# A chain of five layers on one core: another layout of on-chip memory for the split weights and the normed inputs

## The chip, the cores and the metric

The kernel runs on one core of a Trainium2 chip. The metric is the device time of one execution in microseconds (us). TensorE (PE) multiplies matrices, VectorE (DVE) and ScalarE (ACT) work on tiles element by element, GpSimd (POOL) takes some smaller work, and SyncE (SP) issues the transfers (DMA) of the weights. Addresses in this text are KB from the start of a partition of the on-chip memory (SBUF); they are read from the two built programs.

## The reference

Five layers follow one another on 512 tokens of width 1024, in 32-bit arithmetic. This is the core of what is computed:

```python
x = first_block(...)                       # gated MLP branch and RWKV7 branch
for layer in range(2):
    a = rms_norm(h, norm_gains[layer, 0])
    m = mla_mixer(a, ...) if layer == 0 else hgrn2_mixer(a, ...)
    h = h + rms_norm(m, norm_gains[layer, 1])
    a = rms_norm(h, norm_gains[layer, 2])
    h = h + rms_norm(sq_relu_mlp(a, mlp_w1[layer], mlp_w2[layer]), norm_gains[layer, 3])

def sq_relu_mlp(h, w1, w2):                # w1: 1024 x 4096, w2: 4096 x 1024
    a = jax.nn.relu(h @ w1)
    return (a * a) @ w2
```

## The kernel before, in words

**Products.** Every large product is made of three: a 32-bit operand is split into a high part (rounded to the type fp32r) and the rest, and `mm3` (lines 181 to 184) issues high by high, high by low and low by high into one accumulator. A product of one block of 128 output columns, 512 tokens and a depth of 1024 is thus 8 chunks of 3 matmuls, 24 in all. A matmul has a moving operand, whose columns stream past, and a stationary one, which is loaded ahead. In the w1 products of the MLPs and in HGRN2's gates the activations move and the weights stand; in the MLP1's w2 product and in HGRN2's values it is the other way round.

**Weights.** `wchunk` (line 186) has a block of weights loaded by a transfer into a tile `raw` (4 KB of each partition, three buffers, pool `wr`). `wsplit` (line 173) then takes the next split slot: ScalarE casts `raw` to `wh` (line 140), VectorE subtracts to get `wl` (line 123). One slot is 8 KB, `wh` and `wl`. A slot can be written again once the last product that reads it is done. Three slots are there all the time; `wpool(2)` at the end of the MLA layer (line 1391) adds two, so that from MLA's output projection on there are five.

**Activations.** A layer's input is kept as eight chunks of 128 features by 512 tokens. There are two sets: `aH`, `aL` (pool `acts`, low addresses) and `bH`, `bL` (pool `acts2`, `new_acts(True)`, line 1085). The set `b` holds the normed input of both MLPs and of HGRN2; `a` holds the outputs of the mixers and the hidden activations of the MLPs.

**Order of work.** MLA's and HGRN2's output projections end in `mixer_out` (line 1394): `gemm_tail` makes four blocks of columns on all 512 tokens and four in two halves of 256 tokens (`gemm_halves`, line 201), so that `norms` (line 1098) can start on the first half: per half and chunk it scales the mixer's output (`mlom`), adds it to the residual (`res`), and splits the normed sum into `bH` (ScalarE) and `bL` (VectorE). Then `mlp` (line 1406) begins: `gemm_halves` on five blocks of columns of w1 (line 1488), whose accumulators are four `mm` tiles and one `sm` tile; it asks for five split weights before its first matmul in program order. 27 more w1 blocks follow as whole products of 512 tokens, between the w2 products. In MLP1, `second` (line 1442) asks for four split weights for each half of the output width. HGRN2's values take four per half as well.

The instructions of each engine are put in order by a scheduler that works from its own estimates of time; each engine then works through its list in that order.

**Memory.** Pools are stacked from both ends: constants, `acts`, `wr`, the split slots and the MLPs' own tiles from the low end, the residual, `acts2` and the mixers' tiles from the high end. With five slots and the MLPs' tiles both stacks together fill the memory.

Of the kernel before, what the change touches and what calls it, by code (L numbers as in the profile page):

```python
# [11 lines left out]
F32R = mybir.dt.float32r  # L12
# [8 lines left out]
P = 128  # L21
T = 512
# [13 lines left out]
SB = 1  # L36
MB = 1
BEGUN = 1
TT = ("sm", "sm", "mm", "mm")
NFILL = 61  # L40
ORDER = "r0 A0 k1 g0 k2 r1 g0 n0 r2 f11 g0 f1 t0 g1 m0 g1 k3 g1 g2 l0 g2 r3 g3 l1 g2 f7 l2 g3 l3 f2 l4 g3 l5 f5 l6 l7"
# [20 lines left out]
class Kern:  # L62
# [1020 lines left out]
            self.tt(acc[:, s], acc[:, s], sq, ALU.add, self.nc.gpsimd if k < 7 else None)  # L1083

    def new_acts(self, second=False):
        pool, t = (self.ap2, "b") if second else (self.ap_, "a")
        return [(self.tl(pool, [P, T], t + "H", F32R), self.tl(pool, [P, T], t + "L", F32R)) for _ in range(8)]

    def rstd(self, out, sums, n, fac=None):

# [42 lines left out]
    def gemm_tail(self, w, acts, K, evac, norm, begun=()):  # L1133
# [3 lines left out]
        for i in range(len(begun), 4):  # L1137
            self.gemm(w, i * P, acts, K, evac, i)
        self.gemm_halves(w, [i * P for i in range(4, 8)], acts, K, evac, range(4, 8), norm, TT)

# [11 lines left out]
    def mla(self):  # L1152
# [234 lines left out]
            self.psums([("mm", 2), ("sm", 4)], 1)  # L1387
        wx.close()
        self.mlx.close()
        self.wpool(2)  # L1390
        self.ap2 = self.ctx.enter_context(self.pool("acts2", 8))
        self.mixer_out("mlo", w_o, Acts(oa), 1, 2, begun)

    def mixer_out(self, nm, w_o, o, gpost, gpre, begun=()):
# [131 lines left out]
    def hgrn(self):  # L1526
# [3 lines left out]
        with ExitStack() as ox:  # L1530
            oa = self.new_acts()
            with ExitStack() as mx:
# [199 lines left out]
                w_o = I["hgrn_w_o_2"][0]  # L1732
                begun = [self.products(w_o, i * P, Acts(oa), 8, "mm") for i in range(BEGUN)]
                self.psums([("mm", 2), ("sm", 4)], 1)
        self.mixer_out("hgm", w_o, Acts(oa), 5, 6, begun)

    def build(self):
        tc, ctx = self.tc, self.ctx
        self.consts()
        self.sp = ctx.enter_context(self.pool("small", 2, side="left"))  # L1740
        self.ap_ = ctx.enter_context(self.pool("acts", 8, side="left"))
        self.WU, self.leng, self.wprio = 8 * P, self.nc.vector, 400
        self.wr = ctx.enter_context(self.pool("wr", 3, side="left"))
        self.wx = []
        self.wslots, self.wn = [], 0
        self.wpool(3)
        self.block1()
        self.mla()
        self.mlp(0)
        self.hgrn()  # L1750
        self.mlp(1)
# [33 lines left out]
```

## Time and profile before

| | us |
|---|---|
| median of three runs (lowest, highest) | 1616.99 (1616.04, 1617.93) |
| the profiled execution, its own time | 1615.6 |
| its span, first to last instruction | 1613.8 |
| TensorE busy | 1542.8 |
| VectorE busy | 939.0 |
| ScalarE busy | 713.3 |
| GpSimd busy | 329.5 |

In the trace MLA's output projection ends at 605 us, MLP0 at 965, HGRN2 at 1244, and MLP1 goes to the end. A matmul's record in the trace is longer than the time that it takes from the next one, since matmuls overlap; what a matmul costs in a stream without gaps is the distance from its start to the start of the next. In the rows, a name without its number stands for all tiles of a kind: `mm<-bH,wh` is a matmul into an `mm` accumulator with a `bH` tile moving and a `wh` tile standing. Each row ends, in brackets, with the idle time before it and what ended it, if there was any.

### The profile page before, as it was taken

Reading aid. Unit: us, or ns where it says so; the run is one execution under the profiler, and the core shown is the slowest. Engines: PE = TensorE matmul, PEld = TensorE weight load, DVE = VectorE, ACT = ScalarE, POOL = GpSimd, SP = SyncE. Lnnn points to the kernel's source line nnn. Section 1 sums busy time; section 2 is a strip of 40 time slices with the busy share of each in tenths; the row PEclk is TensorE's granted clock in tenths of the full one; section 3 lists DMA queues with packets and bytes.
Section 4 is the critical chain, followed back from the end, with each engine's and each line's share of the span. In section 5 each row is a group of like instructions: output and inputs, shape, how many; then the busy total and the mean of one; then the engine's idle time right before and its main releaser. Section 6 shows DMA issues by size and latency. Waiting matters only on the chain. (4 is left out here: it accounts for less than half of the span.)

```text
span 1613.8 us, 21901 instructions
## 1 busy us (share of the span) xinstructions
PE 1542.8 (96%) x8293; PEld 1305.5 (81%) x8293; DVE 939.0 (58%) x1644; ACT 713.3 (44%) x1297; POOL 329.5 (20%) x459
## 2 busy tenths in 40 slices
PE   5987979999999999999999999999999999999998
PEld 4766768889978899888888887888888988888886
DVE  7797595678667739334343447667754824333445
ACT  3533314655565646333232335667745624322232
POOL 4464732224310023000000033223323200000000
PEclk9998989999999999999999999999999999999999
DMA  9732445544123132333333322322213223231421
GB/s 289 215 97 86 78 130 144 178 132 119 51 70 94 29 105 80 104 103 93 91 93 104 92 91 67 104 79 66 66 53 110 87 79 118 74 110 66 123 86 53
DMA packets 272893, 161.69 MB, mean 100 GB/s; under 512 B 29465, under 2 KB 253316, under 8 KB 272788
## 3 DMA queue, kind: packets, MB, share of 16 engines
q1 hardware_dynamic: 271492, 157.33, 34.2%
q0 software_dynamic: 1152, 2.70, 0.5%
q8 instruction: 65, 1.06, 0.3%
q14 instruction: 40, 0.33, 0.1%
q10 hardware_dynamic: 144, 0.26, 0.0%
HBM read 147.42 MB, written 11.53 MB: 98 GB/s over the span
## 5 line engine op out<-in xcount | busy, mean ns | idle before, releaser
L140 ACT CAST wh<-raw 128x1024 fp32r<-128x1024 f32 (+3 forms) x244 | 242.8, 996 | 466.0 <-PE mm L143 371.2
L123 DVE TENSOR_TENSOR wl<-raw,wh 128x1024 fp32r<-128x1024 f32 (+2 forms) x228 | 272.6, 1197 | 288.1 <-ACT wh L140 284.0
L143 PE MATMUL mm<-bL,wh 128*128 128x512 f32 (+1 forms) x752 | 282.2, 378 | 1.0 <-DVE bL L133 1.0
L143 PE MATMUL mm<-bH,wl 128*128 128x512 f32 (+1 forms) x752 | 281.7, 377 | 0.0
L143 PE MATMUL mm<-bH,wh 128*128 128x512 f32 (+1 forms) x752 | 279.4, 379 | 0.1
L143 PE MATMUL mm<-aH,wh 128*128 128x512 f32 (+1 forms) x656 | 241.0, 369 | 12.3 <-DVE gt L133 9.5
L143 PE MATMUL mm<-aH,wl 128*128 128x512 f32 (+1 forms) x656 | 236.8, 362 | 1.4 <-DVE wl L123 1.4
L143 PE MATMUL mm<-aL,wh 128*128 128x512 f32 (+1 forms) x656 | 237.7, 364 | 0.0
L143 PEld LDWEIGHTS mm<-bL,wh 128*128 128x128 f32 x752 | 141.1, 188 | 29.4 <-DVE bL L133 1.8
L143 PEld LDWEIGHTS mm<-bH,wl 128*128 128x128 f32 x752 | 141.1, 188 | 27.7
L143 PEld LDWEIGHTS mm<-bH,wh 128*128 128x128 f32 x752 | 139.2, 188 | 28.0 <-ACT hg_vt L137 0.5
L143 PEld LDWEIGHTS mm<-aH,wh 128*128 128x128 f32 x656 | 125.2, 191 | 34.4 <-DVE gt L133 10.5
L143 PEld LDWEIGHTS mm<-aH,wl 128*128 128x128 f32 x656 | 125.2, 191 | 20.7 <-DVE wl L123 1.9
L143 PEld LDWEIGHTS mm<-aL,wh 128*128 128x128 f32 x656 | 125.7, 192 | 18.3 <-issue 0.7
L143 PE MATMUL mm<-wh,aH 128*128 128x512 f32 x288 | 113.5, 396 | 1.5 <-ACT aH L140 1.5
L143 PE MATMUL mm<-wh,aL 128*128 128x512 f32 x288 | 112.8, 393 | 0.0
L143 PE MATMUL mm<-wl,aH 128*128 128x512 f32 x288 | 112.6, 393 | 0.0
L140 ACT CAST aH<-t 128x512 fp32r<-128x512 f32 (+1 forms) x74 | 41.1, 564 | 75.7 <-DVE t L123 75.5
L123 POOL TENSOR_TENSOR mlpt<-mlpt,sq 128x256 f32<-128x256 f32 (+1 forms) x9 | 11.9, 1320 | 306.6 <-ACT sq L137 306.6
L245 POOL TENSOR_TENSOR mlpss<-mlpss,pwm 128x1 f32<-128x1 f32 x4 | 2.2, 547 | 322.0 <-DVE mlpss L128 322.0
L123 DVE TENSOR_TENSOR aL<-t,aH 128x512 fp32r<-128x512 f32 (+1 forms) x74 | 45.1, 617 | 36.2 <-ACT aH L140 36.2
L143 PEld LDWEIGHTS mm<-wh,aH 128*128 128x128 f32 x288 | 54.6, 190 | 12.7 <-ACT aH L140 1.9
(545 smaller groups left out, 2819.7 us busy)
## 6 DMA issues: line engine op xcount, KB each, us to landing
raw<-in_mlp_w_dram SPq DMA_DIRECT2D x128, 512.0 KB
raw<-in_hgrn_w_in_dram SPq DMA_DIRECT2D x32, 512.0 KB
raw<-in_w_in_dram SPq DMA_DIRECT2D x23, 512.0 KB
ada<-in_w_ada_dram SPq DMA_DIRECT2D x16, 512.0 KB
raw<-in_w_out_dram SPq DMA_DIRECT2D x10, 512.0 KB
raw<-in_w_ada_dram SPq DMA_DIRECT2D x8, 512.0 KB
raw<-in_mla_w_o_dram SPq DMA_DIRECT2D x8, 512.0 KB
raw<-in_hgrn_w_o_dram SPq DMA_DIRECT2D x8, 512.0 KB
```

The lines of the kernel that those rows point to most:

```text
L123: self.st((eng or self.nc.vector).tensor_tensor(out=out, in0=a, in1=b, op=op))
L140: self.st(self.nc.scalar.copy(out=out, in_=in_))
L143: i = self.nc.tensor.matmul(out, l, r, start=start, stop=stop, **kw)
L245: self.nc.gpsimd.tensor_tensor(out=out, in0=a, in1=cst[: a.shape[0], :n], op=ALU.pow)
```

## The change

Three pools are laid out in another way. The raw weights (`wr`) go to the high end. From MLA's output projection on there is one split slot more than the three, not two, so four in all. `acts2` is divided: five chunks of `bH` and `bL` go to a new pool `acts2l` at the low end, three and the tiles `bs` stay at the high end. No instruction is added or removed on any engine.

```diff
--- before.py
+++ after.py
@@ -36,6 +36,7 @@
 SB = 1
 MB = 1
 BEGUN = 1
+LOW = 5
 TT = ("sm", "sm", "mm", "mm")
 NFILL = 61
 ORDER = "r0 A0 k1 g0 k2 r1 g0 n0 r2 f11 g0 f1 t0 g1 m0 g1 k3 g1 g2 l0 g2 r3 g3 l1 g2 f7 l2 g3 l3 f2 l4 g3 l5 f5 l6 l7"
@@ -1083,8 +1084,8 @@
             self.tt(acc[:, s], acc[:, s], sq, ALU.add, self.nc.gpsimd if k < 7 else None)
 
     def new_acts(self, second=False):
-        pool, t = (self.ap2, "b") if second else (self.ap_, "a")
-        return [(self.tl(pool, [P, T], t + "H", F32R), self.tl(pool, [P, T], t + "L", F32R)) for _ in range(8)]
+        pools, t = ([self.ap2l] * LOW + [self.ap2] * (8 - LOW), "b") if second else ([self.ap_] * 8, "a")
+        return [(self.tl(z, [P, T], t + "H", F32R), self.tl(z, [P, T], t + "L", F32R)) for z in pools]
 
     def rstd(self, out, sums, n, fac=None):
 
@@ -1387,8 +1388,11 @@
             self.psums([("mm", 2), ("sm", 4)], 1)
         wx.close()
         self.mlx.close()
-        self.wpool(2)
-        self.ap2 = self.ctx.enter_context(self.pool("acts2", 8))
+        self.wpool(1)
+        self.ap2 = self.ctx.enter_context(self.pool("acts2", 8 - LOW))
+        self.wx.append(ExitStack())
+        self.wslots.append([])
+        self.ap2l = self.wx[-1].enter_context(self.pool("acts2l", LOW, side="left"))
         self.mixer_out("mlo", w_o, Acts(oa), 1, 2, begun)
 
     def mixer_out(self, nm, w_o, o, gpost, gpre, begun=()):
@@ -1740,7 +1744,7 @@
         self.sp = ctx.enter_context(self.pool("small", 2, side="left"))
         self.ap_ = ctx.enter_context(self.pool("acts", 8, side="left"))
         self.WU, self.leng, self.wprio = 8 * P, self.nc.vector, 400
-        self.wr = ctx.enter_context(self.pool("wr", 3, side="left"))
+        self.wr = ctx.enter_context(self.pool("wr", 3))
         self.wx = []
         self.wslots, self.wn = [], 0
         self.wpool(3)
```

Where the tiles lie in the MLPs and in HGRN2, in KB:

| | before | after |
|---|---|---|
| `aH`, `aL` | 17.75 to 49.75 | the same |
| `raw` | 49.75 to 61.75 | 211.97 to 223.97 |
| split slots | 61.75 to 101.75 (five) | 49.75 to 81.75 (four) |
| `bH`, `bL`, chunks 0 to 4 | 171.97 to 203.97 (with 5 to 7) | 81.75 to 101.75 |
| `bH`, `bL`, chunks 5 to 7 | | at the high end, from 179.97 |

The shift of the residual and the mixers' tiles by 12 KB moves some tiles of block 1 and MLA across the middle of the memory too: most of MLA's eight input tiles `zH`, from 102.84 up before, come to lie below 102.

The order of the instructions changes in two places at the entry of each MLP. **TensorE at the entry of the first MLP**, before: the first row of the fifth block of w1 columns (accumulator `sm_1142`; the four others are `mm_1138` to `mm_1141`, and `wh_1136`, `wl_1137` are its split weights), and the end of the entry.

```order
L143 MATMUL mm_1141_6313<-bH_1038_5745,wh_1133_6300 128x256
L143 MATMUL sm_1097_6193<-ident_66,mlow_5766 128x128 x2
L143 MATMUL sm_1142_6314<-bH_1030_5737,wh_1136_6306 128x256
L143 MATMUL mm_1138_6310<-bL_1039_5746,wh_1124_6282 128x256
L143 MATMUL mm_1138_6310<-bH_1038_5745,wl_1125_6283 128x256
L143 MATMUL mm_1139_6311<-bL_1039_5746,wh_1127_6288 128x256
...
L143 MATMUL mm_1141_6313<-bL_1045_5752,wh_1133_6300 128x256
L143 MATMUL mm_1141_6313<-bH_1044_5751,wl_1134_6301 128x256
L143 MATMUL sm_1142_6314<-bH_1030_5737,wh_1136_6306 128x256
...
L143 MATMUL mm_1166_6622<-bH_1030_5737,wh_1164_6618 128x512
```

In the changed kernel, the end of the entry:

```order
L144 MATMUL mm_1140_6315<-bH_1044_5754,wl_1131_6298 128x256
L144 MATMUL mm_1141_6316<-bL_1045_5755,wh_1133_6303 128x256
L144 MATMUL mm_1141_6316<-bH_1044_5754,wl_1134_6304 128x256
L144 MATMUL sm_1142_6317<-bH_1030_5740,wh_1136_6309 128x256
L144 MATMUL sm_1142_6317<-bL_1031_5741,wh_1136_6309 128x256
L144 MATMUL sm_1142_6317<-bH_1030_5740,wl_1137_6310 128x256
...
L144 MATMUL sm_1142_6317<-bH_1044_5754,wl_1137_6310 128x256
L144 MATMUL sm_1142_6317<-bH_1030_5740,wh_1136_6309 128x256
...
L144 MATMUL mm_1166_6625<-bH_1030_5740,wh_1164_6621 128x512
```

Before, the fifth block's 24 matmuls on the first 256 tokens are strewn among those of the four others, and 24 on the second half stand at the end. Now all 48 stand at the end, behind the last matmul of the other four.

**ScalarE at the same place**, before: the cast of the fifth block's weights, `wh_1136`, and that of the next block, `wh_1164`, with the norm's last activations (`bH_1044`, `sqh_1105`) ahead of it.

```order
L137 ACTIVATE bH_1032_5739<-res1_563_3122,pc_632 128x256
L137 ACTIVATE sqh_1085_6030<-res1_563_3122 128x256
L140 CAST wh_1136_6306<-raw_1135_6304 128x1024
L140 COPY mlom7_5764<-mm_1077_5901 128x256
...
L137 ACTIVATE sqh_1105_6245<-res7_569_3128 128x256
L140 CAST aH_1155_6463<-t_1157_6465 128x256
L140 CAST wh_1164_6618<-raw_1163_6616 128x1024
L137 ACTIVATE t_1158_6495<-mm_1138_6310 128x256
L140 CAST wh_1172_6664<-raw_1171_6662 128x1024
```

In the changed kernel:

```order
L138 ACTIVATE bH_1044_5754<-res7_569_3128,pc_632 128x256
L138 ACTIVATE sqh_1105_6248<-res7_569_3128 128x256
L141 CAST wh_1136_6309<-raw_1135_6307 128x1024
L141 CAST wh_1164_6621<-raw_1163_6619 128x1024
L141 CAST wh_1172_6667<-raw_1171_6665 128x1024
L141 CAST wh_1179_6705<-raw_1178_6703 128x1024
L138 ACTIVATE t_1157_6468<-sm_1142_6317 128x256
```

The cast of `wh_1136` has moved from the middle of the norm to behind its last activation: with four slots it takes the one of the first block (`mm_1138`), while before it took a slot that MLA's output projection had freed. VectorE's subtraction `wl_1137` moves with it. The entry of the second MLP changes in the same way.

## Rows read from the trace of the kernel before

**Rows 1.** The page: busy time by engine, 40 slices, chain by line.

```profile
PE 1542.8 (96%) x8293; PEld 1305.5 (81%) x8293; DVE 939.0 (58%) x1644; ACT 713.3 (44%) x1297; POOL 329.5 (20%) x459
...
PE   5987979999999999999999999999999999999998
...
PEclk9998989999999999999999999999999999999999
...
PE mm L143 19%; DVE mlpy L123 0%; PE sm L143 0%; DVE mlpy L133 0%; PE sm L149 0%; ACT t L137 0%; POOL mlpss L245 0%; DVE mlpss L123 0%; DVEq L1781 0%; POOLq L1781 0%; DVE mlpss L133 0%; DVE mlpss L128 0%; ACTq L137 0%
```

**Rows 2.** Stretches, TensorE: us, busy us (count), granted clock, DMA share, GB/s.

```profile
665.97:698.61 32.64, 32.64 (x145) 1.00 0.40 111
704.21:737.81 33.60, 33.60 (x145) 1.00 0.33 95
1304.46:1309.90 5.44, 5.44 (x25) 1.00 0.00 0
1005.12:1015.63 10.51, 10.51 (x47) 1.00 0.25 68
```

**Rows 3.** Groups by form, TensorE: count, busy us, mean ns, idle before.

```profile
L143 PE MATMUL mm<-bH,wh 128*128 128x512 f32 x624 | 248.7, 399 | 0.1
...
L143 PE MATMUL mm<-wh,bH 128*128 128x512 f32 x64 | 25.2, 399 | 1.4 <-ACT bH L137 1.4
```

**Rows 4.** Timeline of TensorE: start us, duration us; bounds of two half products.

```profile
587.20 0.28 PE L143 MATMUL mm<-aH,wh 128*128 128x256 f32 x1
...
590.08 0.28 PE L143 MATMUL mm<-aH,wh 128*128 128x256 f32 x1
...
634.57 0.28 PE L143 MATMUL sm<-bH,wh 128*128 128x256 f32 x1
...
637.41 0.40 PE L143 MATMUL mm<-bH,wh 128*128 128x512 f32 x1
```

**Rows 5.** Stretch, MLP0 entry: us; PE, PEld, DVE, ACT, POOL busy; clock; DMA.

```profile
605.30:632.40 27.10, 25.48 (x208) 24.65 (x208) 26.47 (x58) 16.44 (x42) 12.81 (x14) 1.00 0.14 40
```

**Rows 6.** Timeline of VectorE, MLP0 entry.

```profile
608.07 1.76 DVE L123 TENSOR_TENSOR wl<-raw,wh 128x1024 fp32r<-128x1024 f32 x1
...
627.78 0.41 DVE L123 TENSOR_TENSOR t<-t 128x256 f32<-128x256 f32 x1
...
631.23 0.42 DVE L123 TENSOR_TENSOR bs<-bs,sqh 128x256 f32<-128x256 f32 x1 [0.63 <-POOL bs L123]
631.57 0.87 DVE L133 SCALAR_TENSOR_TENSOR bL<-res,pc,bH 128x256 fp32r<-128x256 f32 x2
...
634.09 1.23 DVE L123 TENSOR_TENSOR wl<-raw,wh 128x1024 fp32r<-128x1024 f32 x1 [1.25 <-ACT wh L140]
```

**Rows 7.** Timelines of ScalarE and TensorE, MLP0 entry.

```profile
633.00 1.05 ACT L140 CAST wh<-raw 128x1024 fp32r<-128x1024 f32 x1 [1.96 <-PE mm L143]
...
632.11 0.38 PE L143 MATMUL mm<-bL,wh 128*128 128x256 f32 x1 [0.17 <-DVE bL L133]
...
632.80 0.39 PE L143 MATMUL mm<-bH,wl 128*128 128x256 f32 x2
```

**Rows 8.** Timelines of VectorE and TensorE, MLP1 entry.

```profile
1270.04 0.88 DVE L133 SCALAR_TENSOR_TENSOR bL<-res,pc,bH 128x256 fp32r<-128x256 f32 x2
...
1275.88 0.40 PE L143 MATMUL mm<-bH,wh 128*128 128x512 f32 x1
```

**Rows 9.** Timelines of ScalarE and VectorE, first half change of w2 in MLP1.

```profile
1312.87 1.05 ACT L140 CAST wh<-raw 128x1024 fp32r<-128x1024 f32 x1 [0.35 <-PE mm L143]
...
1317.93 1.05 ACT L140 CAST wh<-raw 128x1024 fp32r<-128x1024 f32 x1 [1.80 <-DMA raw<-in_mlp_w_dram]
...
1313.96 2.59 DVE L123 TENSOR_TENSOR wl<-raw,wh 128x1024 fp32r<-128x1024 f32 x2 [0.18 <-ACT wh L140]
```

**Rows 10.** Waits of TensorE, 525 to 565 us: total us, times, longest us.

```profile
PE sm L143 <- ACT P L137: 1.1, 1, 1.1
```


## The prediction, made before the changed kernel was run

> **What bounds the kernel now.** I first read the page. TensorE is busy for 1542.8 us of the span of 1613.8, in the slices from the fifteenth on at nine tenths or more, and its clock stands at the upper of its two levels, 2.4 GHz, in nearly all slices; the parts of the chain that ended last which the page names by line are TensorE's matmuls of line 143 almost alone [rows 1]. So from MLA's output projection on, time is the number of matmuls times the distance between their starts, plus TensorE's few gaps. The change leaves the number of instructions as it is. It can act in three ways: on that distance, on the gaps where a split weight comes too late, and on what TensorE finds to do in a gap.
>
> Then I measured the distance in stretches without a gap. Six w2 products of MLP0, with `aH` and `aL` moving, take 32.64 us for 144 matmuls, 226.7 ns each; six w1 products, with `bH` and `bL` moving, 33.60 us, 233.3 ns [rows 2]. (A count in those rows holds one or two matmuls more, which had begun before.) The clock is 1.00 in both, the weights are of the same five slots, and the form is the same. What differs is where the moving tile lies: `a` up to 49.75 KB, `b` from 171.97 up. Two more stretches set the rule: in MLP1's w2 product the slots move, up to 101.75 KB, and `a` stands: 5.44 us for 24, 226.7 ns. In HGRN2's values the slots move too, but `b` stands: 10.51 us for 45, 233.5 ns [rows 2]. So a 512-column matmul costs 6.6 ns more when either operand lies high, and addresses up to 101.75 count as low. The five moved chunks end exactly there, on addresses that slots held before, and the trace has those at the low price.
>
> The Trainium skill speaks against this: "TensorE: Matmul & The Clock Gate", section "Wait — 56ns, not 53.3ns?", gives the distance from the number of columns and the clock alone, 215.7 ns at 512 columns, with no term for the address. By that rule the layout would bring nothing at the matmuls, and only the lost slot would be left. The trace does not agree with it: 226.7 and 233.3 ns stand side by side at one clock [rows 2].
>
> **The sum, part by part.**
>
> *Five chunks at the low end, whole products.* 624 matmuls of `bH` by `wh` with 512 columns, and as many of each of the two other forms, are 1872, or 78 products of 24: 27 in each MLP, 24 for HGRN2's gates [rows 3]. A product costs 5.60 us high and 5.44 low; five eighths of its matmuls change, 0.10 us. 78 times 0.10 is **7.8 us** less. HGRN2's values are 64 times three, 192 matmuls [rows 3]; 120 of them change, 120 times 6.6 ns is **0.8 us** less. All of it lies on TensorE's path. Bounds: nothing, if one high chunk among eight spoils the product, to 8.6; I take the upper end, because the price follows each matmul's operands in all four stretches.
>
> *The same for the halves.* A half product of 256 columns takes 2.88 us from `a` (587.20 to 590.08) and 2.84 from `b` (634.57 to 637.41) [rows 4], so here low is dearer, by 1.7 ns a matmul. The MLPs' first five blocks are 2 times 5 times 48, 480 matmuls, of which 300 change: **0.5 us** more, between nothing and 0.5.
>
> *One slot less, at the entry of the MLPs.* This is the price. VectorE, working through the norm, is busy for 26.47 of 27.10 us there, TensorE for 25.48 [rows 5]: the norm sets the pace, and TensorE used its spare time for the fifth block's first half. Before, the last `bL` lands at 632.44 (631.57 and 0.87) [rows 6] and the entry ends 4.97 us later, at 637.41 [rows 4]. In the changed kernel the fifth block has no slot until `mm_1138` is done. VectorE's list holds as many `wl` ahead of the last `bL` as before (that of 608.07 is then the fourth block's) and one `t` less, 0.34 us [rows 6], so the last `bL` but one lands at about 631.7. Behind it, in TensorE's order, stand 14 matmuls up to `mm_1138`'s last, at 0.118 us [rows 4]: 633.4. The cast began 0.2 us after that matmul's start (632.80 to 633.00) [rows 7], so now at 633.6; 1.05 later it is done, VectorE takes 1.23 more [rows 6, 7], and at about 635.95 the fifth block's third matmul, the first by `wl`, can go. 46 matmuls at 0.118 are 5.4 us: the entry ends at 641.4, **4.0 us** later. The entry of MLP1 has the same shape, 1270.92 to 1275.88, 4.96 us [rows 8], so both cost **8.0 us**. Bounds for one entry: 2.5, when only the 2.84 us of the half that lost its cover less the `t` come out, to 4.6, if VectorE, which now has `t` earlier in its list, waits once more for 0.6 us as it does at 631.23 [rows 6]. I take 4.0, since each step of it has a row.
>
> *One slot less, elsewhere.* At w2's half changes in MLP1 four split weights are wanted at once, and four slots are left. The last of the four is cast at 1317.93, when its transfer lands, not when a slot comes free, so it stays; the first three shift by one release, 1.36 us, and the first `wl` then ends at about 1315.2 (1313.96 and 1.23) [rows 9], just ahead of the first matmul by it, at 1315.8 (1309.90 and 5.44 of a product, two matmuls on) [rows 2]. Nothing, then; at most one such step late at each of seven changes, some 0.5 us each, 3.5. At HGRN2's entry the four values' weights shift by one release as well; nothing, or one `wl` of 1.23 us on the norm's path. In whole products a cast and a subtraction, 2.3 us [rows 6, 7], fit well within the three products of 5.5 us that other slots hold.
>
> *MLA's tail.* The output projection's second block gets a fresh slot, so some of its matmuls move forward into the attention's tail, where TensorE waits for 1.1 us once [rows 10]. I take **0.4 us** less, between 1.1 less and 0.5 more, if the cast comes ahead of a softmax step.
>
> *Raw weights at the high end.* VectorE and ScalarE read them there; no row has that at another address. Nothing; at most the 0.5 just named.
>
> Sum: 7.8 and 0.8 and 0.4 less, 0.5 and 8.0 more, **0.5 us less**: 1615.1 for the profiled execution of 1615.6. The median of the runs stands 1.4 above that execution, at 1616.99, so I forecast **1616.5**: no change. (Some 0.2%, 3.2 us, is what a measurement of this kernel can tell from none.)
>
> **The rivals.**
>
> *The entries cost less, and it is faster.* If the fifth block's slot comes free earlier than I read, or the shorter list lets the norm end earlier, each entry costs 2.5: the sum is 3.5 less, and with the whole 1.1 at MLA's tail 4.2: **1612.8**. For it: VectorE's spare time at the entry is only 0.6 us, so each instruction that leaves its list counts. Against: the chain of cast, `wl` and 46 matmuls has no slack in it.
>
> *The low price does not come, and it is slower.* If one high chunk in eight keeps the whole product at 5.60 us, or the price hangs on something else than the address, the 8.6 us go and 8.1 stay: **1625**. It decides at the first whole w1 product: 5.60 us or 5.50. Against: rows of either role of the operand agree. The skill's rule above would end here too.
>
> *Slots are short elsewhere.* HGRN2's entry and w2's half changes cost 1.2 and 3.5: 4.7 on top of the sum: **1621**. For it: the margin at a half change is 0.6 us. Against: the scheduler has put other blocks' matmuls between.
>
> **How the numbers follow.** My forecast gets 0.43; the cheaper entries 0.32, the missing low price 0.13, the shortage elsewhere 0.12. So faster 0.32, within 0.2% 0.43, slower 0.25. The forecast's own bounds (entries 2.5 to 4.6 each, tail 1.1 less to 0.5 more) give 1613 to 1619. With the neighbouring cases the range goes from 1611.5 to 1622.5; it leaves out the missing low price and extremes, under 2 in 10.
>
> **What would show it.** Whole w1 products at 5.50 us (a matmul 226.7 ns on five chunks, 233.3 on three) confirm the gain; 5.60 refutes it, 5.44 would mean that the edge lies elsewhere. At MLP0's entry the stretch from the last `bL` to the first 512-column matmul should grow from 4.97 to about 9.3 us, with TensorE waiting for `wl` once. A gap of over 0.3 us at 1315 or at each half change after it speaks for the third rival. If the gain is there and the entry is not longer, my reading of the slots is wrong.

## The result, and the profile after

The changed kernel takes 1634.68 us (median of four runs, 1632.57 to 1635.60), the kernel before 1617.46 in the same comparison: a ratio of 1.0102, 95% interval 1.0084 to 1.0120. It is slower by some 17 us; I had forecast 1616.5, within 1611.5 and 1622.5. The span of the profiled execution grew from 1613.8 to 1632.7.

From the page of the kernel after, the lines that answer to [rows 1]:

```profile
PE 1545.9 (95%) x8293; PEld 1310.7 (80%) x8293; DVE 940.7 (58%) x1644; ACT 712.5 (44%) x1297; POOL 329.2 (20%) x459
...
PE   5987889999999998999999999999999899999998
...
PEclk9998989999999999999999999999999999999999
...
PE mm L144 61%; PE sm L144 6%; PE po L144 2%; DVE wl L124 2%; DVE bL L134 1%; PE sc L144 1%; PE mg L144 1%; DVE TV L124 1%; PE sd L144 1%; DVE acc L134 1%; DVE res L124 1%; DVE acc L124 1%; PE ss L144 1%; DVE bz L124 1%; ACT wh L141 1%
```

TensorE is busy 3 us longer, though no matmul was added, and over 15 us more of the span it stands still. Of the chain that ended last, three quarters are now matmuls and 14% VectorE's work. In the slices the loss is faint: the sixteenth and the thirty-second, which hold the two entries of the MLPs, fall from 9 to 8.

The start of each product in both traces tells where the offset between them arises (how much later the changed kernel starts the same product). It is 0.6 us at the end of block 1 and 1.6 when the first w1 matmul of MLP0 starts (605.35 and 606.92). At the end of that entry it is 11.2, and falls to 8.9 through MLP0 and to 7.4 through HGRN2's gates. HGRN2's output projection takes it to 9.4, MLP1's entry to 20.9, and MLP1's products bring it down to 18.9. So both entries lose, 9.6 and 11.5 us where I had 4.0 each, HGRN2's output projection loses 2.0, and the products win some 6.

Stretches of TensorE, as [rows 2]: six w1 products, then the last part of MLP0's entry and of MLP1's.

```profile
715.34:748.38 33.04, 33.04 (x145) 1.00 0.34 97
645.70:648.60 2.90, 2.90 (x16) 0.50 0.67 182
1291.50:1296.80 5.30, 5.30 (x25) 0.50 0.32 106
```

The products cost 33.04 us for six where they cost 33.60, 5.51 each: the gain is there, at nearly the size forecast (5.50). The two other stretches are what nobody asked for: the granted clock stands at 0.50, the lower of the two levels, and 256-column matmuls go by at some 213 ns instead of 118.

The entry of MLP0 in the timelines of VectorE, TensorE and ScalarE, as [rows 6, 7]:

```profile
633.99 0.87 DVE L134 SCALAR_TENSOR_TENSOR bL<-res,pc,bH 128x256 fp32r<-128x256 f32 x2
...
637.44 3.50 DVE L124 TENSOR_TENSOR wl<-raw,wh 128x1024 fp32r<-128x1024 f32 x3 [2.52 <-ACT wh L141]
644.05 1.23 DVE L124 TENSOR_TENSOR wl<-raw,wh 128x1024 fp32r<-128x1024 f32 x1 [3.12 <-ACT wh L141]
```

```profile
606.92 0.28 PE L144 MATMUL mm<-bH,wh 128*128 128x256 f32 x1
...
634.52 0.39 PE L144 MATMUL mm<-bL,wh 128*128 128x256 f32 x1 [0.35 <-DVE bL L134]
...
637.46 0.39 PE L144 MATMUL sm<-bH,wh 128*128 128x256 f32 x1 [0.31 <-ACT wh L141]
...
638.72 0.39 PE L144 MATMUL sm<-bH,wl 128*128 128x256 f32 x1 [0.76 <-DVE wl L124]
...
644.36 0.39 PE L144 MATMUL sm<-bH,wh 128*128 128x256 f32 x1 [2.75 <-ACT t L138]
...
648.57 0.63 PE L144 MATMUL mm<-bH,wh 128*128 128x512 f32 x1
```

```profile
633.05 0.40 ACT L138 ACTIVATE sqh<-res 128x256 f32<-128x256 f32 x1
636.36 2.95 ACT L141 CAST wh<-raw 128x1024 fp32r<-128x1024 f32 x3 [2.90 <-PE mm L144]
642.98 1.04 ACT L141 CAST wh<-raw 128x1024 fp32r<-128x1024 f32 x1 [3.67 <-DMA raw<-in_mlp_w_dram]
643.93 0.38 ACT L138 ACTIVATE t<-sm 128x256 f32<-128x256 f32 x1
```

SyncE, which issues the transfers, at the same place:

```profile
638.69 6.98 SPq L162 DMA_DIRECT2D raw<-in_mlp_w_dram  x4
```

The last `bL` lands at 634.86 (633.99 and 0.87). TensorE finishes the four blocks' part of the entry, waits for the cast of the fifth block's weights (0.31) and for its `wl` (0.76), and works through the first half of the fifth block. Up to here it is the chain that I had added up: with the second half behind it at 0.118 us a matmul the entry would end at 644.3, 9.4 us after the last `bL`; I had 9.3. But TensorE then waits 2.75 us for an activation `t`, and ends at 648.57. That `t` is the eviction of the fifth block's first half. In ScalarE's list it stands behind four casts, and the fourth cast waits 3.67 us for a transfer, to 642.98. That transfer was issued at 638.69, when VectorE's first subtraction (637.44 and some 1.2) had just ended.

MLP1's entry, VectorE and TensorE, as [rows 8]:

```profile
1280.28 0.87 DVE L134 SCALAR_TENSOR_TENSOR bL<-res,pc,bH 128x256 fp32r<-128x256 f32 x2
...
1291.50 0.58 PE L144 MATMUL sm<-bH,wh 128*128 128x256 f32 x1 [3.60 <-ACT t L138]
...
1296.79 0.63 PE L144 MATMUL mm<-bH,wh 128*128 128x512 f32 x1
```

15.6 us from the last `bL` (1281.15) to the end, where it was 4.96; the wait for `t` is 3.6 us, and the whole second half goes at the lower clock.

### The profile page after: what moved, and what is told of

Same layout as the page of the kernel before. It is cut to its first block, busy times and chain, and to the rows that moved or that the text cites. A ratio compares the mean times of both kernels' runs of the same rounds, so it can differ in the third digit from the quotient of the medians.

```text
span 1632.7 us, 21900 instructions
## 1 busy us (share of the span) xinstructions
PE 1545.9 (95%) x8293; PEld 1310.7 (80%) x8293; DVE 940.7 (58%) x1644; ACT 712.5 (44%) x1297; POOL 329.2 (20%) x459
## 4 chain that ended last, share of the span: by engine, by line
PE 76%; DVE 14%; issue 3%; DMA 3%; ACT 2%; POOL 1%; SPq 1%; DVEq 0%; POOLq 0%; ACTq 0%
PE mm L144 61%; PE sm L144 6%; PE po L144 2%; DVE wl L124 2%; DVE bL L134 1%; PE sc L144 1%; PE mg L144 1%; DVE TV L124 1%; PE sd L144 1%; DVE acc L134 1%; DVE res L124 1%; DVE acc L124 1%; PE ss L144 1%; DVE bz L124 1%; ACT wh L141 1%
```

## The experiments

My theory after the result had two parts: the lost slot costs some 25 us, and the low chunks give some 7 of them back. And, inside the first part: three raw buffers hold weights that wait for slots, so that the fourth transfer is issued too late, and ScalarE's list passes its delay on. The first five kernels test this, the others the price of a matmul.

**Raw weights at the high end, nothing else**

```diff
-        self.wr = ctx.enter_context(self.pool("wr", 3, side="left"))
+        self.wr = ctx.enter_context(self.pool("wr", 3))
```

> One part alone: only the raw weights go to the high end; five slots, all chunks of the normed input high. Theory (the lost slot costs some 25 us, the low chunks give some 7 back): within 2 us of the kernel before, w1 products at 5.60 us. Rival (raw weights at the high end delay the casts, the subtractions or the transfers): slower by 5 us or more, with longer casts (over 1.05 us) or longer subtractions (over 1.23 us).

Measured: 1618.50 us against 1617.24, ratio 1.0004 (0.9992 to 1.0015), w1 products at 5.60 us. Casts and subtractions of 1024 columns are as long as before (means of 1047 and 1254 ns, before 1049 and 1254). Moving the raw weights costs nothing that can be measured.

**Four slots, nothing else**

```diff
-        self.wpool(2)
+        self.wpool(1)
         self.ap2 = self.ctx.enter_context(self.pool("acts2", 8))
```

> One part alone: four split slots instead of five from the output projection of MLA on, all else as in the kernel before. Theory: about 24 to 26 us slower than before (1641 to 1643), since the entries of the two MLPs cost 9.6 and 11.5 us and both output projections some 2, and nothing comes back. Rival (the loss comes from where the tiles lie, or from the raw weights): slower by less than 12 us.

Measured: 1641.44 us, ratio 1.0141 (1.0125 to 1.0158), 24.2 more than before. The ScalarE timeline at MLP0's entry has the same picture as the changed kernel's, with everything in its old place:

```profile
637.96 2.94 ACT L140 CAST wh<-raw 128x1024 fp32r<-128x1024 f32 x3 [2.89 <-PE mm L143]
644.49 1.04 ACT L140 CAST wh<-raw 128x1024 fp32r<-128x1024 f32 x1 [3.59 <-DMA raw<-in_mlp_w_dram]
645.44 0.38 ACT L137 ACTIVATE t<-sm 128x256 f32<-128x256 f32 x1
```

So the slot alone brings the whole loss, and the layout of the tiles is not needed for it. Against this kernel the changed one is 6.8 us faster, which is what the five low chunks bring.

**The changed kernel with its fifth slot back**

```diff
-        self.wpool(1)
+        self.wpool(2)
         self.ap2 = self.ctx.enter_context(self.pool("acts2", 8 - LOW))
```

> The changed kernel with its fifth slot given back, which takes the room it left free; the five low chunks then lie from 89.75 to 109.75 KB, bH 89.75 to 99.75, bL 99.75 to 109.75. Theory: the entries cost what they cost before (4.97 us from the last bL to the first product of 512 columns), and the time falls by 5 to 7 us against before (1610 to 1612), a w1 product taking 5.49 to 5.53 us, as the edge of the low price lies at 104 KB or above. Rival (the loss has nothing to do with the slots): stays over 1625.

Measured: 1612.69 us, ratio 0.9966 (0.9954 to 0.9978), 4.6 less than before; the expectation was 5 to 7, so it fell just short. Six w1 products, and the entry of MLP0 (last `bL`, first matmul of 512 columns):

```profile
708.31:741.35 33.04, 33.04 (x145) 1.00 0.34 97
```

```profile
635.97 0.87 DVE L134 SCALAR_TENSOR_TENSOR bL<-res,pc,bH 128x256 fp32r<-128x256 f32 x2
...
641.83 0.40 PE L144 MATMUL mm<-bH,wh 128*128 128x512 f32 x1
```

From 636.84 to 641.83 are 4.99 us, the old entry, and the products keep the low price although four of the five `bL` now lie at 101.75 KB and above, up to 109.75. An edge at 104 KB, which I had still allowed for, is refuted.

**Four raw buffers**

```diff
-        return self.tl(self.wr, [P, self.WU], "raw")
+        self.wring.append(self.wring.pop(0))
+        return self.tl(self.wring[-1], [P, self.WU], "raw")
...
+        self.wring.append(self.ctx.enter_context(self.pool("wr2", 1)))
...
+        self.wring = [self.wr] * 3
```

> The changed kernel with a fourth buffer for raw weights from the output projection of MLA on; still four slots. Theory, second half (three raw buffers hold weights that wait for slots, so the fourth transfer starts too late, ScalarE waits for it in its list, and the eviction behind it, for which TensorE waits, comes late): the wait of ScalarE for a transfer at the entries (3.7 and 4.5 us) goes, TensorE's wait for that eviction falls from 2.8 and 3.6 to under 1 us, and the time falls by 5 to 9 us against the changed kernel (1626 to 1630). Rival (the wait is for the eviction itself or the cast in front of it): within 2 us of the changed kernel.

Measured: 1626.99 us, ratio to before 1.0055 (1.0040 to 1.0070), 7.7 less than the changed kernel. ScalarE and TensorE at MLP0's entry:

```profile
638.76 3.89 ACT L141 CAST wh<-raw 128x1024 fp32r<-128x1024 f32 x4 [2.90 <-PE mm L144]
644.04 0.38 ACT L138 ACTIVATE t<-sm 128x256 f32<-128x256 f32 x1 [1.39 <-PE sm L144]
...
644.47 0.38 PE L144 MATMUL sm<-bH,wh 128*128 128x256 f32 x1 [0.47 <-ACT t L138]
...
647.43 0.40 PE L144 MATMUL mm<-bH,wh 128*128 128x512 f32 x1
```

Four casts run without a break, `t` follows at 644.04, TensorE waits for it 0.47 us where it waited 2.75, and the 24 matmuls behind it take 2.96 us instead of 4.21. So at the entries the late transfer, its path through ScalarE's list and the fall of the clock are shown to be one chain with one cause. What is left of the entries is 6.0 us each. In HGRN2's output projection this kernel lost 2.6 us, where the changed one lost 2.0; its clock fell there, though nothing waited for a transfer (last section).

**Two accumulators for the fifth block**

```diff
         for s in HALVES:
+            if len(cols) == 5 and acts.parts is not self.mla_acts and s.start:
+                pss[4] = self.ptl("sm")
```

> The changed kernel, but the fifth block's second half has an accumulator of its own, so that TensorE need not wait for the eviction of the first half, which stands in ScalarE's list behind the cast that waits for a transfer. Theory: TensorE's waits for ScalarE's t (2.8 and 3.6 us) go and the clock stays at its upper level, so that each entry ends 4 to 6 us earlier; 8 to 10 us less than the changed kernel, 1624 to 1627. Rival (with that wait gone TensorE waits as long for the next block's split weights): less than 3 us less.

Measured: 1628.86 us, ratio to before 1.0079 (1.0059 to 1.0099), 5.8 less than the changed kernel: less than expected, more than the rival's 3. Stretches of TensorE over both entries, first this kernel, then the changed one (us, busy us and count, clock, DMA share, GB/s), and one of the waits of this kernel in MLP1's entry:

```profile
636.00:652.00 16.00, 14.24 (x95) 1.00 0.50 134
1282.00:1300.00 18.00, 15.88 (x98) 1.00 0.44 147
```

```profile
636.00:652.00 16.00, 12.18 (x72) 0.89 0.50 132
1282.00:1300.00 18.00, 13.33 (x74) 0.81 0.36 117
```

```profile
PE mm L144 <- ACT t L138: 1.5, 2, 1.3
```

The fifth block's second half no longer waits and the clock stays at 1.00, but the product behind it now waits for an eviction in the same list, 0.6 us at the first entry and 1.3 at the second. The transfer still lands late (ScalarE's cast waits 3.84 us for it at the first entry); the wait was only moved on by one product, and shortened.

**Which property of an address sets the price?** In all kernels so far the cheap tiles lay low. But MLA's input tiles `zH`, of which the change brought several below 102 KB, still cost 231 to 237 ns a matmul there. They begin 96 bytes behind a multiple of 256; `a`, the slots and the five low chunks begin at such a multiple (.75 KB), the high chunks 224 bytes behind one (.96875). So a second theory: not the half of memory, but the offset (taken at first for a multiple of 64 bytes). Two kernels part them.

```diff
 five slots, all chunks high, an empty tile of 32 bytes at the end of memory:
+        self.tl(ctx.enter_context(self.pool("pad", 1)), [P, 8], "pad")
 the changed kernel, an empty tile of 32 bytes under the five low chunks:
+        self.tl(self.wx[-1].enter_context(self.pool("pad", 1, side="left")), [P, 8], "pad")
         self.ap2l = self.wx[-1].enter_context(self.pool("acts2l", LOW, side="left"))
```

> The kernel before, five slots, nothing moved to the low end; only an empty tile of 32 bytes is put at the very end of memory, so that every tile at the high end begins 32 bytes lower, at a multiple of 64 bytes (bH from 171.9375 KB, before 171.96875). Theory A (the price of a matmul hangs on the half of memory that its operands lie in): no change, within 2 us of before, w1 products at 5.60 us. Theory B (it hangs on whether the tile begins at a multiple of 64 bytes; in the kernels so far all low tiles did and all high ones did not): w1 products, HGRN2's gates and its values go to 226.7 ns a matmul, 5.44 us a product; 78 products by 0.16 and 192 matmuls by 6.6 ns are 13.7 us, less 0.8 for the halves: 1603 to 1606.

> The changed kernel with an empty tile of 32 bytes under the five low chunks: they stay low (81.78 to 101.78 KB) but no longer begin at a multiple of 64 bytes. Theory A (low or high): as the changed kernel, w1 products at 5.51 us. Theory B (multiple of 64 bytes): the low chunks lose their price, w1 products at 5.60 us, and the time rises by some 7 us to that of four slots without low chunks, 1640 to 1642.

Measured, low but shifted: 1641.30 us, ratio to before 1.0147 (1.0133 to 1.0161), as four slots without low chunks. High at multiples of 64 bytes: 1613.78, ratio 0.9984 (0.9975 to 0.9993), a little less than before, but by far not the 1603 to 1606 of the second theory. Six w1 products of the kernel with shifted low chunks, then of the one with the tile at the end:

```profile
717.66:751.26 33.60, 33.60 (x145) 1.00 0.33 95
```

```profile
703.54:737.15 33.61, 33.61 (x145) 1.00 0.33 96
```

Low is not enough: 32 bytes take the whole gain away, so the rule of my prediction is wrong. A multiple of 64 bytes is not enough either, at least for the moving operand: w1 products stay at 5.60 us. (HGRN2's values, where `b` stands, went from 233.5 to 229.6 ns, from all their matmuls in the trace.)

**All chunks at multiples of 256 bytes, five slots.** 320 bytes of constants are freed so that both ends can be shifted.

```diff
-        self.pw[-0.5] = c([P, 32], "pwm")
+        self.pw[-0.5] = c([P, 8], "pwm")
...
-        s = self.cp.tile([P, rows], F32, tag=tag, name=tag)
+        s = (self.bp if tag == "pa" else self.cp).tile([P, rows], F32, tag=tag, name=tag)
...
-        w = self.tl(self.sp, [P, 2, 5, 2], "lnw", bufs=1)
+        w = self.tl(self.mla_z, [P, 2, 5, 2], "lnw", bufs=1)
...
+        ctx.enter_context(self.pool("pad", 1)).tile([P, 56], F32, tag="pad", name="pad")
+        ctx.enter_context(self.pool("padl", 1, side="left")).tile([P, 16], F32, tag="padl", name="padl")
```

> The kernel before with five slots and all eight chunks at the high end, whose tiles are moved there so that bH and bL begin at a multiple of 256 bytes, as the low tiles do (171.75 KB, before 171.96875); to make room, 320 bytes of small constants go to block 1's pools or are cut, and the low tiles begin at 17.5 KB instead of 17.75, a multiple of 256 bytes as well. Theory C (a matmul with 512 columns costs 226.7 ns where its operands begin at multiples of 256 bytes, 229 to 235 ns elsewhere, wherever in memory): w1 products at 5.44 us, 78 times 0.16 and 192 times 6.6 ns are 13.7 us, less 0.8 for the halves: 1604 to 1606. Rival (it needs the low half as well): within 4 us of before, w1 products at 5.55 to 5.60 us.

Measured: **1603.73 us**, ratio 0.9912 (0.9897 to 0.9927), 13.5 less than before, the fastest of all kernels here. Six w1 products at the high end:

```profile
704.67:737.31 32.64, 32.64 (x145) 1.00 0.34 99
```

5.44 us a product, the low price [rows 2], at 171.75 KB. So the low half of memory is not needed, and 32 bytes of offset were enough to lose the price there: the offset decides between these kernels.

**Eight offsets in one kernel.** Chunk k of `b` lies 32 k bytes behind a multiple of 256.

> A measurement: the changed kernel with all eight chunks in the low half, chunk k of bH and of bL beginning 32 k bytes behind a multiple of 256 bytes. Theory C: in whole w1 products the three matmuls of chunk 0 cost 226.7 ns each, those of the other seven 229 to 235. If only multiples of 64 (or 128) bytes count: chunks 0, 2, 4 and 6 (or 0 and 4) cost 226.7. If low or high is all: every chunk costs 226.7.

Measured: 1640.55 us in one run, against 1617.18 before. Six w1 products:

```profile
717.32:750.80 33.48, 33.48 (x145) 1.00 0.33 96
```

5.58 us a product. The three matmuls of chunk 0, at a multiple of 256 bytes, cost 233.0, 228.9 and 230.3 ns here (means over the 27 whole w1 products of MLP0, from start to start), no less than others; over all chunks the means lie between 227.3 and 237.3. The expectation failed for chunk 0: beside neighbours at other offsets a tile at a multiple of 256 did not get the low price, while in the changed kernel five such chunks beside three others did. So the price is no property of one tile's offset alone. This kernel differs in one thing more: its edit gives each chunk a pool of its own, so that `bH` and `bL` of a chunk lie side by side, where in the other kernels all `bH` of a pool lie in a row ahead of its `bL`. Which of the two it is, the mixed offsets or this, was not tried, and stays open.

**MLA's operands too.** Two more empty tiles, 128 and 160 bytes, in MLA's pools.

> As e8_aligned, and two empty tiles (128 and 160 bytes) bring the operands of MLA (its input zH and zL, cH and cL, and the queries and keys) to multiples of 256 bytes too. Theory C: some 300 more matmuls of 512 columns at 6 ns less, 1 to 2 us below e8_aligned. Rival: same as e8_aligned within 1 us.

Measured: 1605.32 us, ratio to before 0.9925 (0.9910 to 0.9941), no better than 1603.73. The matmuls did get cheaper (`zH` from 233 to 227 ns, `cH` and `cL` from 232.5 to 229.1, means of those with 512 columns), but these are few, and the time does not show it.

## Why the prediction was wrong, point by point

*The low price of the five chunks* was forecast at 7.8 and 0.8 us, less 0.5 for the halves; measured, 6.8 with four slots (1641.44 to 1634.68) and 4.6 with five (1617.24 to 1612.69). A product came to 5.51 instead of 5.50. The size was nearly right; HGRN2 gave less, 1.6 us for its gates where I had 2.4, and nothing in the end for its values (the offset is 8.9 ahead of them and 9.0 behind them) where I had 0.8. The rule behind it was wrong. I had read that either operand at the high end costs 6.6 ns; every tile that I had compared agreed with the offset as well as with the half of memory, and I did not look for a row in which the two part. MLA's `zH` could have warned me: it lay from 102.84 KB up, hardly above the low tiles and far below `b`, at 231 to 237 ns a matmul, and I counted it among the high ones.

*The entry of the MLPs* is the step that failed: 4.0 us each forecast, 9.6 and 11.5 measured, 13.1 of the 18.2 us by which the time missed the forecast. Of the 9.6, the chain of cast, `wl` and 46 matmuls is 4.4 (9.4 less 4.97), as forecast. The norm itself ended 0.85 us later than the offset that the entry began with; I had 0.34 earlier, from the `t` that leaves VectorE's list. VectorE waited twice at `bs`, 0.95 and 1.04 us. The remaining 4.3 I had not seen: 2.9 of waiting for `t` and 1.4 at the lower clock. I had followed the cast of the fifth block through its own chain, but not asked what is queued behind the casts on ScalarE, and not where their transfers come from. Three raw buffers were held by three weights that waited for slots; the fourth transfer could start only when the first subtraction was done, at 638.7, and its cast at 642.98 held up the eviction. Four raw buffers took 7.7 us away, which shows it.

*MLA's tail* was forecast at 0.4 less. From the end of block 1 to the entry the offset grew by 1.0 us instead. Eighteen more matmuls of the output projection do stand ahead of the last attention product (36, before 18), as I had read, but no time came of it. Nor is the growth the slot's price: it is 0.7 with four slots alone, 0.7 with five slots and only the raw weights moved, and 1.1 with five slots and low chunks. Its cause stays open.

*HGRN2's output projection* was not in the sum at all. It takes four slots in its halves and the begun block a fifth, as MLA's does. It lost 2.0 us in the changed kernel, and 2.9 with four slots alone, where the clock fell in it too. TensorE, before and then after:

```profile
1211.52 0.36 PE L143 MATMUL sm<-aH,wh 128*128 128x256 f32 x1
...
1214.11 0.86 PE L143 MATMUL mm<-aH,wh 128*128 128x512 f32 x3
```

```profile
1220.63 0.96 PE L144 MATMUL mm<-aH,wh 128*128 128x512 f32 x3 [1.49 <-ACT aH L141]
...
1222.99 0.39 PE L144 MATMUL sm<-aH,wh 128*128 128x256 f32 x1
...
1223.98 0.50 PE L144 MATMUL mm<-aH,wh 128*128 128x512 f32 x1 [0.48 <-ACT hgms L138]
```

Before, the begun block's half product fills the time until `aH` is there (21 matmuls from 1211.52 on). In the changed kernel it begins only at 1222.99, TensorE waits 1.49 us for `aH`, and most of the half product is left for later, where it fills no wait.

*w2's half changes and HGRN2's entry* cost nothing in the end, as forecast. The offset rises by 2.1 us in the first w2 products of MLP1 and falls by 2.2 at the second half, with four slots alone as well; TensorE waits for nothing in between, so it is work in another order, and not the gap that the third rival would have shown.

*The rivals.* Two of them ended slower, at 1625 and 1621, and had the direction right by accident: one rested on the low price not coming, which did come, the other on slots that are short at HGRN2's entry and w2's half changes, which cost nothing. None had the 24 us that the slot costs. The rule of the Trainium skill that I set against the trace ("TensorE: Matmul & The Clock Gate", section "Wait — 56ns, not 53.3ns?") has no term for an address. Here 226.7 and 233.3 ns stand at one clock for tiles that differ by 224 bytes of offset (the kernel with all chunks aligned, and the one before), so the measurement decides against it.

## What to carry to other kernels

Ask of a buffer that is taken away not only who needs it, but which other buffers its waiting users hold: here a slot less kept three raw buffers full, which delayed a transfer, which delayed a cast, which delayed an eviction in the same list, for which TensorE stood still and then ran at the lower clock. And before a difference between two groups of tiles is put down to where they lie, list everything in which the groups differ, the offset among it: a row that parts two explanations is worth more than four that fit both. A tile's offset is cheap to choose (here some 320 bytes of constants had to go): with all chunks at multiples of 256 bytes the w1 products of this kernel ran at 226.7 ns a matmul, and it was 13.5 us faster than before.

## What the runs showed of the hardware

A stream of 512-column matmuls of type fp32r ran at 226.7 ns from start to start where all its tiles begin at multiples of 256 bytes of a partition (32.64 us for 144, with the moving tiles at the low end and at the high end), and at some 233.3 ns (33.60 or 33.61 us) where the moving tiles begin 192 bytes behind one, 224 bytes, or partly 32 and partly 224, at a clock of 1.00 in each case. Of 256-column matmuls the reverse holds: 120.0 ns aligned, 118.3 ns at 224 bytes. With eight offsets mixed within a product the means lay between 227.3 and 237.3 ns.

After 2.9 and 3.7 us in which TensorE did almost nothing, behind a stretch that was broken by other waits already, the granted clock was 1.00 for the next eleven matmuls at one entry, then 0.50 for 2.9 us; at the other it was 0.50 for 5.3 us. In the kernel with two accumulators, whose entries have more and shorter waits for evictions, it was 1.00 over both entries.

HGRN2's output projection has waits of 0.85 and 1.49 us in the changed kernel and in the one with four raw buffers. The same stretch of both (us, busy us and count, clock, DMA share, GB/s):

```profile
1216.00:1226.00 10.00, 7.17 (x30) 1.00 0.20 69
```

```profile
1216.00:1226.00 10.00, 7.88 (x28) 0.83 0.30 101
```

The clock stays at 1.00 in the one and stands at 0.50 for 3.4 us in the other, as it does with four slots alone and with two accumulators. So the two waits alone do not tell whether it falls; what decides is not shown here.
